# Sums of squares along rows of x on ScalarE for token groups two to eight, in a hybrid attention and retention layer

## The chip, the cores and the metric

The kernel runs on one core of a Trainium2 chip. The core has a matrix engine (TensorE, PE in the profile), a vector engine (VectorE, DVE), an activation engine (ScalarE, ACT), a general engine (GpSimd, POOL) and a queue engine (SyncE, SP) that issues most transfers between HBM and the on-chip memory SBUF. TensorE writes its results to another on-chip memory, PSUM. PEld is TensorE's loading of weights. Each engine works through its own instructions in order and waits on semaphores for the others. The metric is the time of one execution on the device, in microseconds (us); lower is better.

## The reference, cut to what matters

One layer works on 2048 latent tokens x and 256 context tokens ctx, each of 1024 channels:

```python
mod = jax.nn.silu(c) @ w_ada[i] + b_ada[i]             # the same for c_ctx
shift, scale, gate = mod[:, None, :D], mod[:, None, D:2 * D], mod[:, None, 2 * D:]
h_lat = _rmsnorm(x, norm_g[i]) * (1.0 + scale) + shift  # x * rsqrt(mean(x*x) + EPS) * g
h_ctx = _rmsnorm(ctx, norm_g[i]) * (1.0 + scale_c) + shift_c
y_lat, y_ctx = _mixer(h_lat, h_ctx, w_in[i], ...)       # projections, attention, retention
x = x + gate * y_lat
return _rmsnorm(x, final_norm_g)
```

What matters here is the first normalisation: for each token the sum of the squares of its 1024 channels, from it a reciprocal root, and then h = x * root * A + B with A and B per channel, from `mod`. h goes into all the input projections.

## The kernel before, in words

**Tokens and tiles.** The tokens are cut into nine groups of 256: groups 0 to 7 are x, group 8 is ctx. The host hands x over in two layouts. In `xT` (and `ctxT`) channels are on the 128 partitions and tokens along the row, eight channel slices k 0 to 7; h is made from this one, because TensorE needs the channels on the partitions. In `x` (and `ctx`) tokens are on the partitions and channels along the row; before the change only the end of the kernel reads that one. Two groups make a block of 512 tokens, `blk[b]`: a high part (`hhi`) and a low part (`hlo`, what the rounding of the high part leaves out). Each projection is three matmuls per slice k: high by high weight, low by high weight, high by low weight (`tform`, L363).

**The windows.** `window(b)` makes four projection units of block b, step by step: 32 steps per window, three matmuls in each. In window 0 `STEPS` interleaves the four units; later windows take one unit after the other. Each finished unit is copied from PSUM by ScalarE and DVE (L383, L384) and stored to `kS` by SP. Windows 0 to 3 are x, window 4 is ctx. Window 0 has the adaLN matmuls (`ada_mm`, L311) between its steps: four column quarters u, each of four parts j.

**The plan.** `PLAN` is a list written out by hand: (step, action, arguments). After the matmuls of step n (32 per window, counted through) `run_acts(n)` issues the actions whose step is n, in the order of the list. So PLAN sets the order on every engine. Actions with step -1 come before window 0. They are:

- `x` i: request xT of group i (two transfers of 512 KB); `sq` i: squares of group i and their sums over the slices (`squares`, L198 to L203); `cs`: TensorE sums over the partitions, one column per 128 tokens, by matmuls with a vector of ones (`colsum`, L209);
- `rs` i: mean and EPS on DVE (L214), power -0.5 on POOL (L215), and a copy along the row on DVE (L220); `sp`: TensorE turns it so that each token's root lies in its column on all partitions (`spread`, L227); `mu` i, u: DVE multiplies x by it, half u of the slices (L241);
- `ab` i, u: times A plus B per slice, some on DVE (L272) and some on ScalarE (L274), by `TSQ`; `blk` b: take the tiles of block b; `hl` i, u: ScalarE casts the high half (L279), DVE or POOL subtracts for the low one (L283), by `LOV`;
- `p` k: slice k of h for groups 0 and 1 at once (`prep_first`, L262 to L265);
- `s`, `m`, `ar`, `af`: split a part of the adaLN weights (L298, L300), its matmuls (L311), the copy of a finished row of quarter u (L319: ScalarE for even u, DVE for odd u), and its transposes and A and B (L324 to L332);
- `ws`, `w`, `w2`: split or request weights of the projections.

**Buffers and queues.** The pool `st` has four tiles of 512 KB. They hold raw weights, the squares of groups 2 to 8 (two each), and ctx. A tile is handed on in list order as it becomes free; the next writer waits until its last reader is done. Before window 0 the list `LOADS` fills SP's queue: x of groups 0 to 3, the adaLN weights and two sets of projection weights. Each x that has been turned into h is stored to `hS` (`spill_step`, L253), from eight steps after its `hl`, one store at an odd step; the tiles of x of groups 0 and 1 become block 2's high part, those of groups 2 and 3 its low part, so `hl` of groups 4 and 5 waits for these stores. All of these are on SP's queue, and it issues in order: a transfer that waits for its tile holds up those after it.

## Time and profile before

| | |
|---|---|
| median of three runs | 1360.33 us (1356.68 to 1361.18) |
| the profiled execution, its time | 1357.68 us |
| the profiled execution, its span | 1355.7 us |
| TensorE busy | 1310.1 us, 97% |
| DVE, ScalarE, POOL busy | 61%, 45%, 43% |
| mean granted clock of TensorE | 0.996 |
| DMA | 287.25 MB, 212 GB/s |

A row of the timeline gives the start, the length, the engine, the line of the kernel, the operation with its tiles, and in brackets how long the engine stood idle before it and what ended that. A row of the groups gives the same operation summed: the count, the busy time in us, the mean length in ns, and the idle time before. A row of the stages gives, for a stretch of time, the busy us of PE, PEld, DVE, ACT and POOL, the granted clock of TensorE (1.00 is full speed), the DMA share and GB/s. Matmuls are pipelined and their ends are modelled, so the start of the next one says more than the length of one.

### The profile page before, as it was taken

How to read it: one execution, taken by the hardware profiler on the slowest of the kernel's cores; microseconds unless marked ns; L12 is line 12 of the kernel's file. 1: busy time of each engine (PE TensorE's matmuls, PEld its weight loads, DVE VectorE, ACT ScalarE, POOL GpSimd, SP SyncE). 2: the span in 40 equal slices, each digit the busy share in tenths (PEclk: the TensorE clock that was granted, in tenths of full speed). 3: DMA queues.
4: the chain of work that ended last, by engine and by line, in shares of the span. 5: the costliest groups of instructions: out<-in, count | busy, mean ns of one | idle time of the engine just before them, and what ended most of it. 6: DMA issues, size and time to landing. Idle time of an engine off the chain costs nothing.

```text
span 1355.7 us, 23094 instructions
## 1 busy us (share of the span) xinstructions
PE 1310.1 (97%) x8236; PEld 1146.9 (85%) x8236; DVE 828.3 (61%) x1444; ACT 606.5 (45%) x1259; POOL 579.9 (43%) x569
## 2 busy tenths in 40 slices
PE   6999999999999999999999999999999899999997
PEld 2477899887897788998999889889999789888886
DVE  5687366676766755377767777776654633445345
ACT  4454343343533344455555465556643244333432
POOL 4443101554034664445535474655523154544442
PEclk9999999999999999999999999999999999999999
DMA  9386788464867656978587886666528888555433
GB/s 363 135 279 231 259 313 215 164 210 147 326 182 230 216 203 213 265 210 211 148 225 207 226 224 206 195 181 193 163 90 291 278 290 279 159 163 171 163 121 129
DMA packets 172085, 287.25 MB, mean 212 GB/s; under 512 B 17345, under 2 KB 92225, under 8 KB 170690
## 3 DMA queue, kind: packets, MB, share of 16 engines
q1 hardware_dynamic: 139554, 228.35, 55.8%
q10 hardware_dynamic: 32416, 57.42, 11.8%
q8 instruction: 66, 1.08, 0.3%
q14 instruction: 49, 0.40, 0.1%
HBM read 194.48 MB, written 91.23 MB: 211 GB/s over the span
## 4 chain that ended last, share of the span: by engine, by line
PE 70%; DVE 9%; DMA 8%; POOL 4%; issue 4%; ACT 3%; SPq 1%; ACTq 0%; DVEq 0%; POOLq 0%
PE mm L374 17%; PE mm L671 12%; PE mm L1463 11%; PE mm L363 7%; PE sS L1025 4%; PE tr L1052 3%; PE po L1073 3%; PE mm L1187 2%; PE mm L311 2%; PE tr L1054 2%; PE po L1075 2%; DMA v<-rvS 1%; PE mm L1375 1%; POOL hlo L531 1%; PE mm L1374 1%
## 5 line engine op out<-in xcount | busy, mean ns | idle before, releaser
L374 PE MATMUL mm<-whi,hlo 128*128 128x256 f32 x832 | 228.6, 282 | 1.0 <-DMA hlo<-cS 1.0
L374 PE MATMUL mm<-whi,hhi 128*128 128x256 f32 x768 | 224.3, 292 | 0.0
L374 PE MATMUL mm<-wlo,hhi 128*128 128x256 f32 x768 | 216.8, 282 | 0.0
L1056 ACT CAST pt<-tr 128x640 fp32r<-128x640 f32 (+1 forms) x128 | 95.6, 747 | 160.4 <-PE tr L1054 157.8
L1062 DVE TENSOR_TENSOR pt<-tr,pt 128x640 fp32r<-128x640 f32 (+1 forms) x128 | 114.0, 890 | 78.4 <-ACT pt L1056 77.2
L374 PEld LDWEIGHTS mm<-whi,hlo 128*128 128x128 f32 x832 | 156.6, 191 | 1.4 <-DMA hlo<-cS 1.3
L1045 POOL TENSOR_SCALAR sp<-sp,stt 128x640 f32<-128x640 f32 (+2 forms) x128 | 103.1, 808 | 106.3 <-DVE stt L1044 75.7
L374 PEld LDWEIGHTS mm<-whi,hhi 128*128 128x128 f32 x768 | 146.3, 191 | 0.0
L374 PEld LDWEIGHTS mm<-wlo,hhi 128*128 128x128 f32 x768 | 146.1, 190 | 0.0
L1034 DVE CUSTOM_DVE_ANT_0 sp<-sS,nb 128x640 f32<-128x640 f32 (+2 forms) x128 | 105.6, 825 | 33.4 <-DMA nb<-in_rpb_t_dram 20.7
L1039 ACT ACTIVATE sp<-sp,stt 128x640 f32<-128x640 f32 (+2 forms) x128 | 107.4, 839 | 20.3 <-DVE stt L1034 19.1
L625 POOL TENSOR_TENSOR whi<-st,whi 128x512 fp32r<-128x512 f32 x48 | 62.8, 1330 | 107.7 <-ACT whi L624 107.7
L363 PE MATMUL mm<-hhi,whi 128*128 128x512 f32 x256 | 108.2, 423 | 0.0
L363 PE MATMUL mm<-hlo,whi 128*128 128x512 f32 x256 | 102.0, 399 | 6.0 <-DVE hlo L265 2.1
L1025 PE MATMUL sS<-k,q 128*128 128x256 f32 (+3 forms) x512 | 99.1, 315 | 5.1 <-DVE stt L1034 4.7
L363 PE MATMUL mm<-hhi,wlo 128*128 128x512 f32 x256 | 102.0, 398 | 0.3 <-DVE wlo L347 0.3
L671 PE MATMUL mm<-hhi,whi 128*128 128x512 f32 x336 | 98.1, 395 | 1.6 <-POOL whi L625 1.6
L1463 PE MATMUL mm<-wor,y 128*128 128x512 f32 x384 | 95.7, 398 | 1.1 <-DVE xt L1472 1.1
L1472 DVE TENSOR_TENSOR xt<-mm,xt 128x512 f32<-128x512 f32 x64 | 43.9, 687 | 82.6 <-PE mm L1463 82.5
L1025 PEld LDWEIGHTS sS<-k,q 128*128 128x128 f32 x512 | 82.8, 188 | 12.0 <-DVE stt L1034 8.2
L1463 PE MATMUL mm<-won,y 128*128 128x512 f32 x336 | 89.9, 406 | 0.0
L625 POOL TENSOR_TENSOR wlo<-st,wlo 128x512 fp32r<-128x512 f32 x36 | 53.1, 1476 | 75.8 <-ACT wlo L624 73.7
(258 smaller groups left out, 3051.5 us busy)
## 6 DMA issues: line engine op xcount, KB each, us to landing
st<-in_w_in_dram SPq DMA_DIRECT2D x64, 512.0 KB
q<-qS SPq DMA_DIRECT2D x64, 256.0 KB
hlo<-hS SPq DMA_DIRECT2D x20, 512.0 KB
k<-kS SPq DMA_DIRECT2D x16, 576.0 KB
kS<-o SPq DMA_DIRECT2D x16, 512.0 KB
vB<-o SPq DMA_DIRECT2D x64, 128.0 KB
qS<-o ACTq DMA_DIRECT2D x16, 512.0 KB
woS<-g ACTq DMA_DIRECT2D x32, 256.0 KB
```

What stands on the lines that cost most here:

```text
L363: nc.tensor.matmul(pm[:, :n], ww[:, k, cs], h[:, k, :], start=(k == 0 and i == 0), stop=(k == KC - 1 and i == 2))
L374: nc.tensor.matmul(pm[:, t * WG:(t + 1) * WG], h[:, k, o:o + P], ww[:, k, :], start=(k == 0 and i == 0), stop=(k == KC - 1 and i == 2))
L625: nc.gpsimd.tensor_tensor(t[:, 1], r, f(t)[:, 0], ALU.subtract)
L671: nc.tensor.matmul(pm, ww[:, k, :], hh[:, k, :], start=(k == 0 and i == 0), stop=(k == KH - 1 and i == 2))
L1025: nc.tensor.matmul(o, hd["q"][i][:, hl, j * P:(j + 1) * P], k, start=(hl == 0), stop=(hl == 1))
L1034: nc.vector.tensor_tensor_reduce(T["sp"][:, :n], T["s"], nbz[big][:, o:o + n], -1.0, 3e38, ALU.add, ALU.min, T["st"][:, 0:1])
L1039: nc.scalar.activation(sp[:, :n], sp[:, :n], AF.Exp, bias=st[:, 0:1], scale=-1.0, accum_out=st[:, 1:2])
L1045: nc.gpsimd.tensor_scalar(sp[:, :n], sp[:, :n], st[:, 2:3], 0.0, ALU.mult, ALU.add)
L1056: nc.scalar.copy(pt[:, :ng_ + 2, 0, :], tr[:, :ng_ + 2, :])
L1062: nc.vector.tensor_tensor(pt[:, :n, 1, :], tr[:, :n, :], f(pt)[:, :n, 0, :], ALU.subtract)
L1463: nc.tensor.matmul(pm, yy[:, k, :], ww[:, k, sl], start=(k == 0 and i == 0), stop=(k == 3 and i == 2))
L1472: nc.vector.tensor_tensor(xts[t][:, sl], pm, xts[t][:, sl], ALU.add)
```

## The change

Groups 2 to 8 get their sums of squares in another way. A new action `xt` i requests the group's rows from `x` (or `ctx`), token on the partition, in two transfers of 512 KB into two `st` tiles. `sq` i for these groups is now two ScalarE instructions, Square with an accumulated sum along the row, which leave the sums of 128 tokens each in a column of a small SBUF tile `rs`. The adds on DVE and POOL (L200 to L203) and the column sums on TensorE (L209) stay for groups 0 and 1 alone. `rs` works on that tile in place.

```diff
+    def load_xt_(i):
+        sqs[i] = []
+        src = a["ctx"] if i == 8 else a["x"][i * 256:(i + 1) * 256, :]
+        for t in range(2):
+            xt = env["st"].tile([P, KH, 256], F32, name="st").rearrange("p k t -> p (k t)")
+            nc.sync.dma_start(xt, src[t * P:(t + 1) * P, :])
+            sqs[i].append(xt)
+
     def squares(i):
+        if i >= 2:
+            rms[i] = env["st"].tile([P, 2], F32, name="rs", bufs=4)
+            for t, xt in enumerate(sqs[i]):
+                nc.scalar.activation(xt, xt, AF.Square, accum_out=rms[i][:, t:t + 1])
+            return
         sqs[i] = []
         for u in range(2):
-            sq = xsq[i][u] if i < 2 else env["st"].tile([P, KH, 256], F32, name="st")
+            sq = xsq[i][u]
...
     def rstd(i):
-        r = env["st"].tile([P, 2], F32, name="rs", bufs=4)
+        r = rms[i] if i >= 2 else env["st"].tile([P, 2], F32, name="rs", bufs=4)
```

The plan changes with it, from step 4 on. The rows of groups 2 and 3 are requested right behind `LOADS`, ahead of x of groups 4 and 5; the other rows follow as tiles become free. The `sq` of groups 2 and 3 stand at step 9, ahead of the row copy `ar` 2; before, group 2 stood at step 5 (ahead of `p` 3) and group 3 at step 12. The `rs` and `sp` of groups 2 and 3 come at steps 12 and 13 (before: 15 and 16), and all of block 1's `mu`, `ab` and `hl` at steps 13 to 22, ahead of `p` 7 and `p` 6 in part (before: 17 to 29). ctx is requested at step 32 (before: 79), its rows at step 46. From step 53 on, the actions other than squares, column sums and requests keep their steps.

```diff
-    (-1, 'p', 0), (-1, 'p', 1), (-1, 'm', 1, 3), (-1, 'ws', 1), (0, 'ar', 1), (3, 'af', 1), (4, 'mu', 1, 1),
-    (4, 's', 2, 0), (4, 'x', 4), (4, 'p', 2), (5, 'sq', 2), (7, 'm', 2, 0), (8, 'm', 2, 1), (9, 'p', 3),
-    (9, 'm', 2, 2), (9, 'm', 2, 3), (9, 'ar', 2), (12, 'mu', 0, 1), (12, 'af', 2), (12, 'm', 3, 0), (12, 'sq', 3),
-    (12, 'p', 5), (12, 'm', 3, 1), (12, 'p', 4), (13, 'sq', 4), (13, 'cs', 2, 3), (13, 'm', 3, 2), (14, 'm', 3, 3),
-    (15, 'rs', 2), (15, 'ar', 3), (16, 'rs', 3), (16, 'af', 3), (16, 'sp', 2, 3), (17, 'mu', 3, 0), (18, 'p', 7),
-    (19, 'mu', 2, 0), (20, 'x', 5), (20, 'p', 6), (22, 'mu', 2, 1), (23, 'mu', 3, 1), (23, 'cs', 4), (24, 'ab', 2, 0),
...
-    (31, 'sq', 5), (34, 'mu', 4, 1), (39, 'ab', 4, 0), (42, 'cs', 5), (42, 'rs', 5), (48, 'ab', 4, 1), (50, 'sp', 5),
+    (-1, 'p', 0), (-1, 'p', 1), (-1, 'm', 1, 3), (-1, 'ws', 1), (0, 'ar', 1), (3, 'af', 1), (4, 'xt', 2),
+    (4, 'xt', 3), (4, 'mu', 1, 1), (4, 's', 2, 0), (4, 'x', 4), (4, 'p', 2), (7, 'm', 2, 0), (8, 'm', 2, 1),
+    (9, 'p', 3), (9, 'sq', 2), (9, 'sq', 3), (9, 'm', 2, 2), (9, 'm', 2, 3), (9, 'ar', 2), (10, 'xt', 4),
+    (10, 'x', 5), (11, 'xt', 5), (12, 'mu', 0, 1), (12, 'af', 2), (12, 'm', 3, 0), (12, 'p', 5), (12, 'm', 3, 1),
+    (12, 'p', 4), (12, 'rs', 2), (12, 'rs', 3), (13, 'sp', 2, 3), (13, 'm', 3, 2), (13, 'mu', 2, 0), (13, 'mu', 3, 0),
+    (14, 'm', 3, 3), (14, 'sq', 4), (14, 'ab', 2, 0), (14, 'blk', 1), (14, 'ab', 3, 0), (14, 'hl', 2, 0),
+    (15, 'ar', 3), (15, 'mu', 2, 1), (15, 'xt', 6), (16, 'af', 3), (16, 'hl', 3, 0), (16, 'mu', 3, 1), (17, 'p', 7),
+    (18, 'p', 6), (19, 'ab', 2, 1), (19, 'rs', 4), (20, 'ab', 3, 1), (20, 'sq', 5), (21, 'hl', 2, 1), (21, 'xt', 7),
+    (22, 'hl', 3, 1), (26, 'sp', 4), (26, 'x', 6), (28, 'mu', 4, 0), (30, 'mu', 4, 1), (31, 'sq', 6), (32, 'x', 8),
+    (36, 'ab', 4, 0), (40, 'rs', 5), (42, 'ab', 4, 1), (45, 'sq', 7), (46, 'xt', 8), (48, 'sp', 5), (50, 'mu', 5, 0),
...
+    (55, 'hl', 4, 0), (55, 'hl', 5, 0), (55, 'ab', 5, 1), (60, 'sq', 8), (61, 'hl', 5, 1), (62, 'rs', 6),
+    (68, 'sp', 6), (70, 'rs', 7), (73, 'mu', 6, 1), (73, 'ab', 6, 1), (73, 'hl', 6, 1), (75, 'sp', 7),
```

## The prediction

> **What bounds the kernel now.** I read the busy shares first, then the stages of the first 165 us, then TensorE's idle times there, and last the groups of instructions that the change takes out.

> ```profile
> span 1355.7 us, 23094 instructions
> PE 1310.1 (97%) x8236; PEld 1146.9 (85%) x8236; DVE 828.3 (61%) x1444; ACT 606.5 (45%) x1259; POOL 579.9 (43%) x569
> ```

> TensorE sets the end: 97% busy. The change touches the first five windows alone (0 to about 160 us), so it is worth what it takes from TensorE's idle time, slow clock and extra matmuls there; all later work follows TensorE. By the matmul rows, window 0 runs from 28 to 74 us, window 1 from 74.2, window 2 from 101.2. The idle times (in brackets) that matter:

> ```profile
> 38.46 0.50 PE L363 MATMUL mm<-hlo,whi 128*128 128x512 f32 x1 [1.73 <-DVE hlo L265]
> 49.24 0.41 PE L324 MATMUL mm<-ident,o 4*128 4x4 f32 x4
> 53.92 0.95 PE L209 MATMUL mm<-one,st 128*128 128x1 f32 x8
> 54.79 1.88 PE L311 MATMUL mm<-clo,silc 128*2 128x512 f32 x4
> 61.24 1.33 PE L227 MATMUL mm<-ident,t 128*128 128x128 f32 x8
> 67.27 0.47 PE L363 MATMUL mm<-hlo,whi 128*128 128x512 f32 x1 [0.37 <-DVE hlo L265]
> 76.55 0.47 PE L363 MATMUL mm<-hlo,whi 128*128 128x512 f32 x1 [1.96 <-DVE hlo L283]
> 103.04 0.50 PE L363 MATMUL mm<-hlo,whi 128*128 128x512 f32 x1 [1.45 <-POOL hlo L283]
> 108.47 0.71 PE L227 MATMUL mm<-ident,t 128*128 128x128 f32 x4 [1.51 <-DVE t L220]
> 110.75 0.58 PE L209 MATMUL mm<-one,st 128*128 128x1 f32 x4 [0.17 <-DVE st L203]
> 126.07 0.58 PE L209 MATMUL mm<-one,st 128*128 128x1 f32 x4 [0.15 <-DVE st L203]
> ```

> The stages (busy time of PE, PEld, DVE, ACT, POOL; then TensorE's granted clock, DMA share, GB/s):

> ```profile
> 30.00:40.00 10.00, 7.96 (x33) 4.45 (x32) 8.73 (x13) 4.98 (x8) 8.05 (x5) 0.99 1.03 410
> 40.00:50.00 10.00, 10.00 (x28) 3.58 (x27) 2.87 (x6) 2.48 (x3) 2.09 (x2) 0.84 0.52 206
> 50.00:60.00 10.00, 10.00 (x33) 3.65 (x32) 8.40 (x17) 3.97 (x6) 5.18 (x7) 1.00 0.00 1
> 60.00:70.00 10.00, 9.63 (x50) 7.59 (x49) 8.58 (x18) 5.01 (x10) 3.09 (x4) 1.00 0.00 0
> 70.00:80.00 10.00, 8.04 (x33) 6.28 (x32) 9.19 (x14) 8.45 (x12) 7.28 (x4) 0.86 0.61 183
> 80.00:90.00 10.00, 10.00 (x46) 8.29 (x45) 6.62 (x12) 2.58 (x5) 2.34 (x3) 0.96 1.05 383
> 90.00:100.00 10.00, 10.00 (x48) 8.36 (x47) 9.13 (x12) 6.94 (x10) 5.11 (x4) 1.00 1.03 336
> ```

> The reader is to see three things. The clock falls just after the two longest idle times: 0.84 over 40 to 50 us is a loss of about 1.6 us, and 0.86 with 0.96 after 76.5 us is 1.4 + 0.4 = 1.8 us; after 1.45 and 1.51 us of idle it did not fall. DMA is idle from 45 to 72 us, and full from 74 to 100 us. And DVE is the busy helper (8 to 9 of 10 us) wherever TensorE waits.

> **What is removed.** Seven groups lose their sums of squares on DVE and POOL and their column sums on TensorE:

> ```profile
> L200 POOL TENSOR_TENSOR st<-st 128x512 f32<-128x512 f32 x7 | 10.4, 1484 | 12.9 <-ACT st L198 12.9
> L201 POOL TENSOR_TENSOR st<-st 128x256 f32<-128x256 f32 x7 | 5.8, 832 | 0.5
> L200 DVE TENSOR_TENSOR st<-st 128x512 f32<-128x512 f32 x7 | 5.8, 833 | 0.8 <-ACT st L198 0.8
> L201 DVE TENSOR_TENSOR st<-st 128x256 f32<-128x256 f32 x7 | 3.8, 545 | 0.2
> L203 DVE TENSOR_TENSOR st<-st 128x256 f32<-128x256 f32 x7 | 3.0, 425 | 1.1 <-DVE st L201 0.5
> L209 PE MATMUL mm<-one,st 128*128 128x1 f32 x28 | 3.6, 237 | 0.3 <-DVE st L203 0.3
> ```

> Per group that is 1.80 us of DVE (0.83 + 0.55 + 0.43) and 2.32 us of POOL. On TensorE the eight column sums at 53.92 hold up the next matmul until 54.79, 0.87 us, so a group's four cost about 0.44. All seven: 7 x 0.4 = 2.8 us, straight on the path.

> **What is added.** ScalarE squares as much as before (two 128x1024 per group, 1.05 us each) and also reads an accumulator: 14 x 0.187 us = 2.6 us, hidden, since ScalarE is 45% busy.

> ```profile
> L198 ACT ACTIVATE st<-hlo 128x1024 f32<-128x1024 f32 x4 | 4.0, 1045 | 0.0
> L1419 ACT ACTIVATION_READ_ACCUMULATOR ot<-xt x32: 185/187/224, 1160.8 to 1349.9; 128x1 f32 x32
> ```

> The rows of x are 14 more transfers of 512 KB (7 MB) on SP's queue. At 410 GB/s one takes 1.28 us. Four MB of them fall into the idle 45 to 72 us. What they cost is order, on three queues, in the terms below.

> **Window 0, term by term.** (a) Squares of group two were at step 5, between two steps that feed TensorE; their adds ran on POOL and DVE while DVE made the low half that TensorE awaits at 38.46.

> ```profile
> 34.35 0.40 DVE L263 TENSOR_SCALAR hhi<-hhi,mods 128x256 f32<-128x256 f32 x1
> 36.11 1.37 DVE L263 TENSOR_SCALAR hhi<-hhi,mods 128x256 f32<-128x256 f32 x1
> 37.52 0.90 DVE L265 TENSOR_TENSOR hlo<-hhi 128x256 fp32r<-128x256 f32 x1
> ```

> Without them it is ready near 37.0: the 1.37 us falls to the 0.40 of the same operation before, and the 0.90 to the 0.43 that L203 takes for this size. Gain 1.73 - 0.3 = 1.4, and the slow clock after it, 1.6: together 3.0.

> (b) ScalarE now squares groups two and three *ahead of* the copy of the third modulation row, and waits there for rows that are requested only after all the first loads.

> ```profile
> 31.89 4.11 SPq L190 DMA_DIRECT2D hhi<-in_xT_dram x4
> ```

> The loads before end near 45.1 us (206 GB/s over 40 to 50 is five full us), with x of groups four and five last, these 2 MB; so the old list without these ends at 40.0, and the four transfers of rows two and three at 45.1. With 0.8 us until ScalarE sees it (chosen between 0 and 2), the last square with its read ends at 47.1 and the row copy at 47.7.

> ```profile
> 47.12 0.57 ACT L319 COPY o<-mm 4x512 f32<-4x512 f32 x1 [9.82 <-PE mm L311]
> ```

> So the copy is where it was, but TensorE, 3.0 us earlier by (a), reaches its transposes at 49.24 - 3.0 = 46.2 and waits 1.4. Behind the waiting ScalarE stands nothing but this copy.

> (c) The spread matmuls of groups two and three (61.24 in the old order) come forward to step 13, in place of the column sums at 53.92. Their scales stand on DVE behind the preparation of k 5 and 4 of block 0: the transposes end at 48.0, the modulation rows take DVE 0.7 us, two casts of ScalarE 0.6 each, then DVE four TENSOR_SCALARs (0.4 to 0.6, behind the casts) and two subtractions (0.4 to 0.9), to about 52.4; then per group DVE, POOL, DVE:

> ```profile
> L262 ACT ACTIVATE hhi<-hhi,mods 128x256 fp32r<-128x256 f32 x16 | 8.4, 590 | 12.4 <-DVE mods L332 8.5 <-DVE hhi L241 3.8
> L215 POOL TENSOR_TENSOR rs<-rs,mhalf 128x2 f32<-128x2 f32 x9 | 6.4, 707 | 25.8 <-DVE rs L214 25.8
> L220 DVE COPY t<-rs 128x256 f32<-128x256 f32 x9 | 3.7, 412 | 7.4 <-POOL rs L215 7.4
> L241 DVE TENSOR_TENSOR hhi<-hhi,mm 128x1024 f32<-128x1024 f32 x8 | 9.6, 1210 | 0.5 <-PE mm L227 0.5
> ```

> 1.25 us each, ready at 53.7 and 54.9. TensorE is there at 52.3: it waits 1.4 + 0.7 = 2.1.

> (d) Block 1 is made at once: between the spread and k 6 of block 0 DVE now has four multiplications by the spread (1.21), four pairs of TENSOR_SCALAR (0.4 each), a row copy, a subtraction (1.2) and k 7 and 6 (2.4), about 11.5 us from 55.5, plus 0.5 us of waits: k 6 is ready near 67.5. TensorE is there near 66 and waits 1.5 where it waited 0.37: a loss of 1.1. POOL's low halves of group two run under it.

> Window 0: +3.0 (a) + 0.87 + 0.4 (column sums of groups two, three, four) - 1.4 - 2.1 - 1.1 = -0.3. It ends as late as before; what was won early is waited away.

> **Window 1.** Block 1 is ready by about 72.5, so the 1.96 at 76.55 and the 1.8 of slow clock go: +3.8. The column sums of groups five and six go: +0.8. TensorE reaches window 2 4.2 us earlier, near 97.0.

> **Window 2.** Here the queues decide. SP is in order, and the rows of group seven wait for group five's squares, near 69 us; eight stores of x to hS, five kS stores, x of group six, ctx, then the rows of ctx stand behind: 10.5 MB, of which 9.0 until the last store that frees block 2's low half.

> ```profile
> 72.48 0.63 SPq L151 DMA_DIRECT2D kS<-o  x1
> L283 POOL TENSOR_TENSOR hlo<-hhi 128x1024 fp32r<-128x1024 f32 x2 | 5.7, 2862 | 2.6 <-ACT hhi L279 2.6
> ```

> (Before, that train began at 72.48.) At 410 GB/s the slot is free at 93 us, at the 360 of the rows for 80 to 100 us at 96; two POOL subtractions (2.4 to 2.9 each) follow: 97.8 to 101.0. I take 99.4, a wait of 2.3. ScalarE's squares of ctx wait for rows landing at 97 to 100.6, and the high half of group five's second part is queued behind them: low half 101.4 to 105.1, taken 103.2, a wait of 1.1; then the scales of group six, 1.25 us, a wait of 0.6. Sum 4.0 against 1.45 + 1.51 = 3.0 before: -1.0. DVE and POOL, relieved by 1.8 and 2.3 us per group, would alone have removed both. The last two column sums and their waits give 0.9 + 0.3 = +1.2.

> **Sum.** -0.3 + 3.8 + 0.8 - 1.0 + 1.2 = 4.5 us earlier at window 4, where TensorE has no wait but 1.0 us until 240 us, so it passes to the end. The profiled execution took 1357.68 us; this gives 1353.2. The median shown, 1360.33, lies 2.65 above that execution, and less 4.5 gives 1355.8. The four executions shown spread over 4.5 us, so I take a value between: 1355.0. About 0.3% (4.1 us) is what a measurement of this kernel can tell from no change.

> **Rivals.** (1) *The waits are exchanged, and the clock falls again* (23%): 2.1 us of idle within 3.2 us at (c), and 2.3 at window 2, are as long as those that cost 1.6 to 1.8 before. At (c) part hides in (d), so 1.3 + 1.7 = 3.0 is lost again; gain 1.5, 1358.8 by the median, within 0.3%. For it: the clock fell after 1.73. Against it: not after 1.51, and (c) is in two pieces.

> (2) *The helpers' relief wins* (22%): rows land when needed, block 2 waits for nothing. Without (b), (c)'s first wait and window 2's 4.0 the gain is 4.5 + 1.4 + 1.4 + 4.0 = 11.3; half of it, 8 to 9, is likelier: 1351.5. For it: DMA is empty for 27 us. Against it: ScalarE takes (b)'s rows in order.

> (3) *Slower: the DMA train of window 1* (11%). At the mixed rate of one early microsecond of that train,

> ```profile
> 77.00:78.00 1.00, 1.00 (x5) 0.81 (x4) 1.00 (x2) 1.00 (x2) 1.00 (x1) 0.65 0.91 263
> ```

> 10.5 MB from 69 us land at 111; squares 2.3, cast 1.05, subtraction 1.2, scales 1.25 later the spread of group six starts at 117.7 instead of 108.47: 9.2 later, less the 1.2 of window 3: 8.0 slower, 1368.3. It decides once those rows land after 104 us (break-even) and shows beyond 108.

> (4) *The slow clock does not hang on the two waits* (6%): it falls at 40 us among thin adaLN matmuls and at 77 wherever the first dense window begins, and falls in the new order too. Then the 1.6 and 1.8 stay lost: gain 4.5 - 3.4 = 1.1, 1359.2. For it: two cases are few. Against it: both follow the longest waits within 1 us, and elsewhere neither thin nor dense matmuls are slow. [...]

> (5) That rows summed on ScalarE are not what runs has no support: the same form is in the trace at L1419.

> **Numbers.** Forecast 38% (own range 1352 to 1357.5), rivals (1) to (4) 23, 22, 11 and 6%. Faster by over 0.3%: rival 2 and some 60% of the forecast, 0.45. Within: rivals 1 and 4 and the rest, 0.44. Slower: 0.11. Range 1349.5 to 1361: the unknown rows (DMA 360 or 410 GB/s, +-1.6; the clock, 3.0; (b) to (d), +-2) and most of rivals 1 and 2.

> **What would show it.** Right: no L209 beyond eight instructions; no idle before the low-half matmul that opens window 1, and a clock of 1.00 there; a wait of TensorE on ScalarE's row copy before 48 us; waits on the scale copies near 53 us; window 2 opening on POOL's low half near 99 us. Wrong: ScalarE squaring group two before 43 us, no wait at step 13, k 6 in time, or squares of ctx that wait beyond 104 us.

## The result, and the profile after

The changed kernel took 1365.21 us (median of five runs, 1364.89 to 1368.2) against 1358.52 us for the kernel before (five runs): a ratio of 1.0052, 95% interval 1.0034 to 1.0071. It is about 7 us slower where 4.5 us faster was forecast. The profiled execution took 1365.21 us. In the changed kernel the line numbers have moved: `tform` is L377, the copies of a finished unit L397 and L398, the stores of k L152 and of x to `hS` L267, `hl` L293 and L297, `ab` L286 and L288, `rs` L228 to L234, `spread` L241, the weight splits L359 and L361.

The page's first lines, then TensorE's idle times of the changed kernel:

```profile
span 1363.4 us, 23026 instructions
PE 1308.8 (96%) x8208; PEld 1146.7 (84%) x8208; DVE 814.1 (60%) x1423; ACT 607.8 (45%) x1273; POOL 563.1 (41%) x555
```

```profile
37.30 0.50 PE L377 MATMUL mm<-hlo,whi 128*128 128x512 f32 x1 [0.31 <-DVE hlo L279]
48.15 0.41 PE L338 MATMUL mm<-ident,o 4*128 4x4 f32 x4 [1.62 <-ACT o L333]
54.41 0.71 PE L241 MATMUL mm<-ident,t 128*128 128x128 f32 x4 [1.43 <-DVE t L234]
55.60 0.71 PE L241 MATMUL mm<-ident,t 128*128 128x128 f32 x4 [0.48 <-DVE t L234]
68.69 0.47 PE L377 MATMUL mm<-hlo,whi 128*128 128x512 f32 x1 [1.38 <-DVE hlo L279]
94.31 1.19 PE L241 MATMUL mm<-ident,t 128*128 128x128 f32 x4 [7.43 <-DVE t L234]
107.38 0.50 PE L377 MATMUL mm<-hlo,whi 128*128 128x512 f32 x1
111.50 0.71 PE L241 MATMUL mm<-ident,t 128*128 128x128 f32 x4 [0.51 <-DVE t L234]
...
172.80 0.38 PE L388 MATMUL mm<-whi,chi 128*128 128x256 f32 x1 [1.09 <-ACT whi L359]
174.06 0.39 PE L388 MATMUL mm<-wlo,chi 128*128 128x256 f32 x1 [0.76 <-DVE wlo L361]
```

Stages of the changed kernel (columns as in the prediction):

```profile
40.00:50.00 10.00, 8.38 (x28) 3.13 (x28) 0.67 (x4) 5.87 (x11) 0.00 (x0) 1.00 1.03 410
70.00:80.00 10.00, 10.00 (x48) 8.33 (x47) 7.70 (x8) 2.39 (x4) 2.66 (x2) 1.00 0.68 224
80.00:90.00 10.00, 6.88 (x31) 5.37 (x29) 0.98 (x2) 3.58 (x7) 0.00 (x0) 1.00 1.00 316
90.00:100.00 10.00, 5.68 (x19) 4.73 (x20) 6.75 (x14) 5.38 (x11) 0.70 (x1) 0.66 1.02 325
```

TensorE did less work, as it was to do (28 matmuls fewer). The opening of window 1 is free of waits and the clock there is 1.00. Then comes one wait of 7.43 us, for the scales of group five, and a clock of 0.66 over 90 to 100 us. The trace's clock records have TensorE at half clock from 91.47 to 98.30 us, that is 3.4 us of clock. But 2.84 us of it lie inside the wait, so the matmuls behind the wait lose only about 2.0. Together that is about 9.4 us in the middle of window 1, where the prediction had nothing. Window 1 took 31.8 us here (75.16 to 106.95); in e12 below, which has neither wait nor slow clock in it, it took 22.2.

The chain behind it is read on three engines. SyncE's issues:

```profile
69.88 0.39 SPq L267 DMA_DIRECT2D hS<-hlo  x1
76.18 0.63 SPq L152 DMA_DIRECT2D kS<-o  x1
76.86 1.86 SPq L267 DMA_DIRECT2D hS<-hlo  x1
78.81 1.44 SPq L191 DMA_DIRECT2D chi<-in_xT_dram  x2
80.86 0.60 SPq L152 DMA_DIRECT2D kS<-o  x1
...
93.03 1.99 SPq L267 DMA_DIRECT2D hS<-hlo  x2
```

ScalarE, over the same stretch:

```profile
73.25 1.05 ACT L293 CAST hhi<-hlo 128x1024 fp32r<-128x1024 f32 x1 [2.87 <-DVE hlo L286]
74.20 1.07 ACT L397 CAST o<-mm 128x512 fp32r<-128x512 f32 x2
80.37 0.58 ACT L397 CAST o<-mm 128x512 fp32r<-128x512 f32 x1 [5.10 <-DMA kS<-o]
...
89.09 0.58 ACT L397 CAST o<-mm 128x512 fp32r<-128x512 f32 x1 [6.06 <-DMA kS<-o]
...
100.35 2.95 ACT L293 CAST hhi<-hhi 128x1024 fp32r<-128x1024 f32 x3 [2.13 <-DMA hS<-hhi]
```

Before the change, the first of these copies (L383 there) waited for TensorE alone, and ran five microseconds earlier (DVE's half of it at 71.77, against 75.47 after):

```profile
69.15 0.59 ACT L383 CAST o<-mm 128x512 fp32r<-128x512 f32 x1 [1.44 <-PE mm L363]
```

And DVE in the changed kernel:

```profile
70.35 2.80 DVE L286 TENSOR_SCALAR hlo<-hlo,mods 128x256 f32<-128x256 f32 x2
...
89.71 0.69 DVE L398 TENSOR_TENSOR o<-mm,o 128x512 fp32r<-128x512 f32 x1 [8.04 <-ACT o L397]
...
92.84 0.16 DVE L228 TENSOR_SCALAR rs<-rs 128x2 f32<-128x2 f32 x1
93.87 0.29 DVE L234 COPY t<-rs 128x256 f32<-128x256 f32 x1 [0.88 <-POOL rs L229]
```

Read from the top. With all of block 1 made at once, the cast of group three's second half (73.25) stands on ScalarE ahead of the copy of the first finished unit (74.20). So the first store of k leaves at 76.18 instead of 72.48, and SyncE, which issues in order, stands still from 70.3 until then. The stores of x and the 1 MB of x 6 then go out ahead of the second store of k. The copies go into the pool `op`, which has two tiles, so the fourth copy waits until the second store has landed: 80.86 to about 89. DVE does its half of that copy right behind ScalarE and stands 8.04 us. Behind it in DVE's order are the scales of group five (92.84, 93.87), and TensorE's spread at step 48 needs them.

The second half of the same delay is paid later in SyncE's queue: the last stores of x that free block 2 go out from 92.53 to 95.0. Block 2's casts wait for the one of 92.53, from the tile `hhi`, and begin at 100.35. This is hidden in the changed kernel only because TensorE is itself late.

Three landmarks split the 7.7 us between the two profiled executions (1355.7 and 1363.4). Window 4 (ctx) begins at 153.0 before and 154.4 after: 1.4 us. The first matmul of the later stage with summed weights (called the tail below) begins at 234.3 and 238.9: 3.2 us more, lost inside the stage over ctx, where the two waits for `whi` and `wlo` above and two of 0.36 and 0.76 at 191.7 and 193.0 stand (before, only 0.51 there). From there to the end it is 1121.4 and 1124.5: 3.1 us more, in instructions that did not change.

### The profile page after: what moved, and what is told of

Read it like the earlier page. It is cut to its first block, busy times and chain, and to the rows that moved or that the text cites. A ratio compares the mean times of both kernels' runs of the same rounds, so it can differ in the third digit from the quotient of the medians.

```text
span 1363.4 us, 23026 instructions
## 1 busy us (share of the span) xinstructions
PE 1308.8 (96%) x8208; PEld 1146.7 (84%) x8208; DVE 814.1 (60%) x1423; ACT 607.8 (45%) x1273; POOL 563.1 (41%) x555
## 3 DMA queue, kind: packets, MB, share of 16 engines
q8 instruction: 65, 1.06, 0.3%
## 4 chain that ended last, share of the span: by engine, by line
PE 44%; DMA 6%; POOL 6%; DVE 5%; issue 4%; ACT 3%; ACTq 0%; SPq 0%; POOLq 0%; DVEq 0%
PE mm L1477 11%; PE mm L388 10%; PE sS L1039 4%; PE tr L1066 3%; PE mm L377 3%; PE po L1087 3%; PE mm L1201 2%; PE tr L1068 2%; PE po L1089 2%; DMA woS<-g 1%; DMA v<-rvS 1%; PE mm L1389 1%; PE mm L1388 1%; PE mm L1387 1%; POOL g L773 1%
## 5 line engine op out<-in xcount | busy, mean ns | idle before, releaser
L377 PE MATMUL mm<-hhi,whi 128*128 128x512 f32 x256 | 108.2, 423 | 0.0
L377 PE MATMUL mm<-hlo,whi 128*128 128x512 f32 x256 | 102.0, 398 | 2.1 <-DVE hlo L279 1.7
L377 PE MATMUL mm<-hhi,wlo 128*128 128x512 f32 x256 | 102.0, 399 | 0.3 <-DVE wlo L361 0.3
L1477 PEld LDWEIGHTS mm<-wor,y 128*128 128x128 f32 x384 | 69.9, 188 | 18.4 <-issue 3.5
```

Source lines behind the costliest of these rows:

```text
L377: nc.tensor.matmul(pm[:, :n], ww[:, k, cs], h[:, k, :], start=(k == 0 and i == 0), stop=(k == KC - 1 and i == 2))
L1477: nc.tensor.matmul(pm, yy[:, k, :], ww[:, k, sl], start=(k == 0 and i == 0), stop=(k == 3 and i == 2))
```

## The experiments

All ratios are to the kernel before, with 95% intervals; it had a median of 1358.52 us beside the changed kernel, and of 1359.4 to 1359.8 us beside the experiments. The last columns are the start of window 4, of the tail, and the distance between, each from the profiled execution. No kernel leaves out any of the computation.

| kernel | ratio | window 4 | tail | between |
|---|---|---|---|---|
| before | 1 | 153.0 | 234.3 | 81.3 |
| changed | 1.0052 [1.0034, 1.0071] | 154.4 | 238.9 | 84.5 |
| e1 | 1.0066 [1.0042, 1.0090] | 157.4 | 242.6 | 85.2 |
| e2 | 1.0106 [1.0077, 1.0135] | 161.0 | 247.7 | 86.7 |
| e3 | 1.0027 [1.0011, 1.0043] | 155.2 | 237.2 | 82.0 |
| e4 | 1.0071 [1.0043, 1.0099] | 160.6 | 243.5 | 82.9 |
| e5 | 1.0038 [1.0022, 1.0055] | 154.9 | 240.9 | 86.0 |
| e6 | 1.0015 [0.9999, 1.0030] | 150.8 | 238.0 | 87.2 |
| e7 | 1.0067 [1.0043, 1.0091] | 156.2 | 243.3 | 87.1 |
| e8 | 1.0019 [0.9999, 1.0039] | 153.2 | 236.1 | 82.9 |
| e9 | 1.0001 [0.9984, 1.0019] | 153.3 | 234.3 | 81.0 |
| e10 | 0.9986 [0.9966, 1.0005] | 150.4 | 231.9 | 81.5 |
| e11 | 1.0058 [1.0035, 1.0080] | 155.1 | 242.1 | 87.0 |
| e12 | 1.0034 [1.0018, 1.0051] | 155.5 | 235.9 | 80.4 |
| e13 | 0.9998 [0.9983, 1.0013] | 151.9 | 233.7 | 81.8 |
| e14 | 1.0020 [1.0008, 1.0032] | 154.4 | 235.5 | 81.1 |
| e15 | 1.0015 [1.0000, 1.0031] | 154.8 | 235.6 | 80.8 |
| e16 | 1.0043 [1.0028, 1.0057] | 156.7 | 238.3 | 81.6 |
| e17 | 0.9988 [0.9973, 1.0003] | 150.8 | 232.1 | 81.3 |
| e18 | 0.9978 [0.9963, 0.9992] | 149.1 | 230.4 | 81.3 |

### e1: the scales of group five out of the wait

```diff
-    (40, 'rs', 5)
+    (22, 'rs', 5)
```

> The changed kernel with the scales of group five (rs 5) at step 22 in place of 40, so that DVE does them before it waits for any copy of a finished unit. Theory A (SP's one queue: stores of x to hS stand behind kS stores, so block 2's tiles come free late, at 100.4 us): the 7.4 us wait before the spread of group five goes, but TensorE then waits at the opening of window 2 for the low half that POOL ends near 107 us; time within 2 us of the changed kernel's 1365. Rival B (only the place of rs 5 in DVE's order): 7.4 us of idle and 3.4 us at half clock go, 1355.

Measured: 1367.43 us, 0.4 us above what theory A allowed. The wait of 7.43 is gone, and TensorE's idle times in the timeline of e1 now are:

```profile
105.97 0.80 PE L377 MATMUL mm<-hhi,whi 128*128 128x512 f32 x1 [7.61 <-ACT hhi L293]
109.90 0.80 PE L377 MATMUL mm<-hlo,whi 128*128 128x512 f32 x1 [3.13 <-POOL hlo L297]
```

The scales were late only because DVE stood in the copy. Taking them out does not help, because block 2 is late from the same cause: its casts wait for a store of x (ScalarE, 2.80 us at 102.98).

### e2: the stores of k on ScalarE's own queue

```diff
-            if b == 4 and n == 0:
+            if b == 0 and n == 0:
                 env["queue"] = nc.scalar
```

> The changed kernel with the kS stores of windows 0 to 3 issued by ScalarE's queue in place of SP's. Theory A: SP no longer stands behind copies that are not done, the hS stores go out at their steps (before 80 us, in place of up to 95), block 2's tiles are free before 93 us, no wait over 2 us in windows 1 and 2; 1353 to 1356. Rival C (7 MB more for the DMA engines, whatever the order): the waits stay, 1363 to 1366.

Measured: 1373.86 us, the slowest of all and outside both ranges; the expected gain did not come. ScalarE's timeline in e2:

```profile
84.68 0.59 ACT L397 CAST o<-mm 128x512 fp32r<-128x512 f32 x1 [6.46 <-DMA kS<-o]
```

SyncE no longer stands still: it issues stores of x from 70.64 to 78.88. But the first store of k is issued at 76.96 (76.18 in the changed kernel), among them, and the third copy waits for its landing until 84.68. ScalarE now also waits for DVE's half of a copy before it can issue the store, up to 5.27 us at a time. So the place in SyncE's queue is only a part of the cause, and e2 brought a cost of its own; it does not tell the two apart.

### e3 and e4: rows without the new order, the new order without rows

e3 keeps rows and sums on ScalarE, but puts the scales and all of h of groups two to four back at the old steps. e4 keeps the sums of the kernel before (groups three and five are squared earlier) and makes the block at once. Of each edit some entries are shown.

```diff
e3:
-    (13, 'mu', 2, 0), (14, 'ab', 2, 0), (14, 'hl', 2, 0), (22, 'hl', 3, 1)
+    (19, 'mu', 2, 0), (24, 'ab', 2, 0), (28, 'hl', 2, 0), (29, 'hl', 3, 1)
...
e4, against the kernel before:
-    (16, 'sp', 2, 3), (19, 'mu', 2, 0), (24, 'ab', 2, 0), (29, 'hl', 3, 1)
+    (13, 'sp', 2, 3), (13, 'mu', 2, 0), (14, 'ab', 2, 0), (22, 'hl', 3, 1)
```

> Rows and ScalarE sums as in the changed kernel, but scales, multiplications and h of groups two to four at the steps they had before (15 to 48), so h of block 1 is not made at once. If the rows are the cause (rival C): a wait of 5 us or more in window 1 or 2 stays, 1362 or more. If making h at once is the cause (it puts block 1's last casts ahead of the first copy of a unit, so the first kS store and all behind it go out 3.7 us later): no such wait, the 2 us at the opening of window 1 come back, 1356 to 1360.

> The kernel before with its sums on DVE, POOL and TensorE, but the steps of the changed kernel for groups two to five: h of block 1 at once, squares of group three at step 9, of five at 20. No rows are loaded. If making h at once delays the first kS store and the train behind it (theory A): a wait of over 4 us for group five's scales or at the opening of window 2, 1361 or more. If the rows are the cause (rival C): neither wait, 1354 to 1358.

Measured: e3 1363.64 us, e4 1367.34 us. TensorE's timeline in e4:

```profile
97.27 1.20 PE L227 MATMUL mm<-ident,t 128*128 128x128 f32 x4 [8.11 <-DVE t L220]
```

e4 has the wait, without one row loaded. So the order of h makes it, and the 7 MB of rows are not needed for it. e3 has no such wait, but it does not come back to the kernel before either: 1356 to 1360 was expected, and its ratio is 1.0027 [1.0011, 1.0043]. Its window 1 opens with waits of 1.07 and 1.48 us and a clock of 0.81 and then 0.85, much as in the kernel before, and at 104.20 and 108.71 us it waits 2.02 and 1.68 us for block 2. The second of these is the one that the prediction's account of window 2 had: ScalarE stood 3.47 us for the rows of ctx, and a cast of block 2 stood behind. So the rows have a cost of their own, smaller than that of the order.

### e5 and e8: copies that need not wait for a store

Window 0's four copies get four tiles that lie idle by then, instead of the two of `op`; e8 does the same in the kernel before.

```diff
-        o = op.tile([P, 2, 512], F32R, name="o")
+        o = wad[8 + own.pop(0)].bitcast(F32R) if b == 0 else op.tile([P, 2, 512], F32R, name="o")
```

> The changed kernel, where the four copies of window 0's finished units go to four tiles that are free then (those of the adaLN weights of quarter 2), not to the two that each kS store must leave first. Theory D (the fourth copy waits for the landing of the second kS store, DVE waits in order for that copy, and group five's scales and SP's stores behind the fourth kS store wait with it): the 8.0 us idle of DVE and the 7.4 us of TensorE go, the last stores that free block 2 go out before 90 us in place of 95; 1352 to 1358. Rival E (the DMA engines are full from 78 us, the landing only shows it): a wait of over 5 us moves to the opening of window 2, 1362 or more.

> The kernel before with the four copies of window 0's units in tiles of their own as in e5. There ScalarE waits 4.0 us for a landing before the fourth copy (83.09), but TensorE waits for nothing behind it; theory D: within 2 us of the kernel before, as what bounds it is DVE between 92 and 107 us.

Measured: e5 1364.45 us (rival E's time), e8 1361.18 us. In e5 DVE's 8 us at the fourth copy are gone, and ScalarE and TensorE read:

```profile
99.08 2.94 ACT L293 CAST hhi<-hhi 128x1024 fp32r<-128x1024 f32 x3 [9.77 <-DMA hS<-hhi]
```

```profile
102.07 0.79 PE L377 MATMUL mm<-hhi,whi 128*128 128x512 f32 x1 [4.53 <-ACT hhi L293]
106.00 0.80 PE L377 MATMUL mm<-hlo,whi 128*128 128x512 f32 x1 [3.14 <-POOL hlo L297]
```

The shared tiles make the first wait, and the late train of stores makes the second; removing one shows the other. In the kernel before, neither bites: its waits stayed as they were (1.97 and 1.45).

### e6: the first copy ahead of the second halves

```diff
-    (19, 'ab', 2, 1), (20, 'ab', 3, 1), (21, 'hl', 2, 1), (22, 'hl', 3, 1)
+    (25, 'ab', 2, 1), (25, 'ab', 3, 1), (25, 'hl', 2, 1), (25, 'hl', 3, 1)
```

> The changed kernel with the second halves of block 1 (ab and hl, half 1, of groups two and three) at step 25, behind the copy of the first finished unit (step 24), in place of steps 19 to 22. Theory D with its start in the crowding: the first copy runs near 72 us in place of 74.2 and the first kS store near 73 in place of 76.2, so the fourth copy waits about 3 us less; TensorE's wait falls from 7.4 to 3 to 5 us, a wait of up to 2 us for block 1's second half comes at step 36; 1359 to 1364. If the crowding is not the start: as the changed kernel, 1365.

Measured: 1360.76 us. The first store of k goes out at 72.71, and window 4 begins at 150.8, 2.2 us ahead of the kernel before. TensorE's idle times in e6:

```profile
91.07 0.68 PE L241 MATMUL mm<-ident,t 128*128 128x128 f32 x4 [2.96 <-DVE t L234]
...
171.15 0.58 PE L388 MATMUL mm<-whi,chi 128*128 128x256 f32 x1 [3.06 <-ACT whi L359]
172.41 0.58 PE L388 MATMUL mm<-wlo,chi 128*128 128x256 f32 x1 [0.46 <-DVE wlo L361]
```

So what stands ahead of the first copy starts the chain. And what was won there was lost again in the stage over ctx, with a clock of 0.66 over 170 to 180 us: the second loss, larger here than in the changed kernel.

### e7: x of group six later

```diff
-    (26, 'x', 6)
+    (44, 'x', 6)
```

> The changed kernel with x of group six (1 MB) requested at step 44 in place of 26, so it does not stand between the first and the second kS store on SP. Theory D: the second kS store goes out some 1.5 us earlier and lands some 3 us earlier, the fourth copy and TensorE's wait shrink by 3 us; 1360 to 1363. If the landing does not decide: 1365.

Measured: 1367.69 us (theory D: 1360 to 1363). TensorE's wait at the scales of group five falls to 3.18 us, but 2.28 and 0.76 us and smaller ones come up after 104 us, and 3.1 in the stage over ctx. ScalarE stands 4.08 us for the rows of ctx at 106.33 there. That the moved request is what delays them was not tested by itself.

### e9, e10, e14: the second loss

In the stage over ctx the copies of window 4 again wait for stores of k. Behind them on ScalarE is the split of the next weights. ScalarE in the changed kernel:

```profile
168.10 0.37 ACT L397 CAST o<-mm 128x256 fp32r<-128x256 f32 x1 [4.26 <-DMA kS<-o]
...
170.28 0.37 ACT L397 CAST o<-mm 128x256 fp32r<-128x256 f32 x1 [1.80 <-DMA kS<-o]
...
171.70 1.99 ACT L359 CAST whi<-st 128x1024 fp32r<-128x1024 f32 x2 [1.05 <-DVE o L398]
```

The kernel before has one such wait there, a shorter one:

```profile
165.83 0.37 ACT L383 CAST o<-mm 128x256 fp32r<-128x256 f32 x1 [3.27 <-DMA kS<-o]
```

At that time SyncE reads 2 MB of h back (`hhi` from `hS`, issued at 156.55 in the changed kernel). The edit puts these four requests behind the next request for weights, which waits for its tiles, so they go out at 165.57 in e14; e9 has it on the kernel before, e14 on the changed one, e10 on e6.

```diff
-            if b == 4 and n % 8 == 0:
-                raw_piece(0, n // 8)
...
     load_w()
+    for n in range(4):
+        raw_piece(0, n)
     w0 = wr[3]
```

> The kernel before, with one edit: the four requests that read 2 MB of stored h back (hhi from hS, issued by SyncE at 155.2 to 157.6 in the kernel before, while the stores of k of the window over ctx go out) stand behind the request for weights that SyncE holds until 172.5. Theory A (the read-back slows the stores of k, whose landing holds ScalarE's copies, and these hold the split of the next weights): ScalarE's waits for kS landings in that window fall from 3.27 us to under 1.5, the wait of 0.51 for whi at 171.1 goes, and the time falls by 0.5 to 1.5 us, unless the read-back is now late for its first use at 188.3. Rival C (stores and weights are late for another reason): those waits stay within 0.5 us and the time is the same.

> The changed kernel with the second halves of groups two and three behind the first copy (as in e6) and the read-back of h behind the held request for weights (as in e9). Window 4 should begin at 150.8 as in e6, 2.2 us before the kernel before. Theory A: TensorE's waits of 3.06 and 0.46 for whi, and the slow clock over 170 to 180, go; the tail begins 3 to 4 us earlier than in e6 (234 instead of 238) and the time falls from 1360.8 to 1356 to 1358, under the kernel before. Rival C (what is won ahead of window 4 is lost there in any case, because the weights come when they come): a wait of 2 us or more for whi stays, and the time stays within 1 us of 1360.8.

> The changed kernel with the read-back of h behind the held request for weights (as in e9) and nothing else. It sizes the second loss by itself: window 4 should begin at 154.4 as in the changed kernel. If what was lost behind window 4 (84.5 us from its start to the tail, against 81.3 before) comes from the read-back, the waits of 1.09, 0.76, 0.36 and 0.76 for whi go, the distance to the tail falls to 81 to 82 and the time by 2.5 to 3.5 us, to 1361.5 to 1363; what stays over the kernel before is then window 1's share. If it does not come from there: the distance stays at 84 or more and the time is 1365.

Measured: e9 1359.18 us, e10 1357.09 us (not to be told from the kernel before), e14 1362.72 us. TensorE in e10:

```profile
90.72 1.19 PE L241 MATMUL mm<-ident,t 128*128 128x128 f32 x4 [3.03 <-DVE t L234]
...
174.32 0.38 PE L388 MATMUL mm<-wlo,chi 128*128 128x256 f32 x1 [0.67 <-DVE wlo L361]
```

The distance from window 4 to the tail falls from 87.2 to 81.5 (e6 to e10) and from 84.5 to 81.1 (changed to e14). In all nine kernels that have the edit it lies between 80.4 and 81.8; without it, between 81.3 and 87.2. In e14 the same copy of ScalarE, at 166.11, waits 2.16 us for TensorE and no longer for a store. So the read-back is what takes the 3.2 us, and theory A holds where there was something to lose. In e9 the wait for the store goes too, but the kernel before lost only 0.51 us there and the time stays (0.5 to 1.5 us less was expected). Why its weights are in time behind a wait of 3.27 us, and those of the changed kernel late, was not tested.

### e11 and e12: with ctx moved back as well

Both have e5's and e6's edits and ctx at the old steps; e12 has the later read-back too.

```diff
-    (32, 'x', 8), (46, 'xt', 8), (60, 'sq', 8)
+    (79, 'x', 8), (80, 'xt', 8), (86, 'sq', 8)
```

> The changed kernel with three edits: second halves of groups two and three behind the first copy (e6), window 0's copies into tiles of their own (e5), and the requests and sums for ctx (x 8, xt 8, sq 8) back at the steps of the kernel before (79, 80, 86). Theory A (the chain of late stores and the two shared copy tiles cause the first loss, whole): no wait over 1 us on TensorE between 75 and 120, and window 4 begins at 149 to 150.5. The time then depends on what the stage over ctx gives back: with waits for whi of 3 to 5 us as in e6, 1358 to 1361. Rival: a wait of over 2 us stays somewhere between 75 and 120, because the order of h itself leaves too much work ahead of each unit; time 1360 to 1364.

> e11 with the read-back of h behind the held request for weights as in e9 and e10. Theory A in both places: no wait over 1 us between 75 and 120, none for whi over 0.5 us after 160, and the forecast's gain arrives: 1353 to 1356, against about 1359.5 for the kernel before. Rival C: the wait for whi stays and the time is that of e11 within 1 us.

Measured: 1366.59 and 1363.7 us, both outside every range. Half of theory A's expectation came: no wait over 0.9 us from 75 to 120 us, and window 1 at its shortest, 22.2 us. The other half did not, because of this edit itself. TensorE and ScalarE in e12:

```profile
128.81 0.80 PE L377 MATMUL mm<-hhi,whi 128*128 128x512 f32 x1 [6.13 <-ACT hhi L293]
```

```profile
123.65 1.06 ACT L207 ACTIVATE st<-st 128x1024 f32<-128x1024 f32 x1 [6.75 <-DMA st<-in_ctx_dram]
```

Rows that are requested six steps ahead hold ScalarE for 6.75 us, and the casts of block 3 stand behind. Sums on ScalarE from their own copy of the rows need the early request. The sums of the kernel before, from the tiles that x is in anyway, don't.

### e13, e15, e16: both causes removed, and ctx between the trains

e13 is e10 with e5's tiles. e15 is e13, and e16 is e10, with ctx at other steps:

```diff
-    (32, 'x', 8), (46, 'xt', 8), (60, 'sq', 8)
+    (64, 'x', 8), (64, 'xt', 8), (80, 'sq', 8)
```

> The changed kernel with three edits: second halves of groups two and three behind the first copy (e6), window 0's copies into tiles of their own (e5), the read-back of h behind the held request for weights (e9); the rows of ctx stay at the changed kernel's steps (32, 46, 60). Theory A: the wait of 3.03 us for group five's scales and the 1.7 us of half clock behind it, which e10 keeps, go too; no wait over 1.5 us between 75 and 240; window 4 begins at 146 to 149 and the tail at 227 to 231; time 1351 to 1355, faster than the kernel before. Rival D (with own tiles the stores of the second block of h become the next limit, as in e5): a wait of 2 to 5 us at the opening of window 2 takes the place of the one removed, window 4 begins at 150 to 152, time 1356 to 1359.

> e13 with the four requests for ctx (2 MB) at step 64 instead of 32 and 46, and the sums over its rows at step 80 instead of 60: SyncE then sends them at about 108, behind the stores of the second block of h, and ten steps ahead of their use. Theory A (in e13 the train of requests on SyncE between 72 and 98 is the limit, and ctx's 2 MB stand in it): the stores of h end by 93 instead of 96, the waits of 1.07 and 3.44 us at the opening of window 2 fall under 1 us together and the half clock behind them goes; ScalarE's wait for ctx rows stays under 1 us (6.75 in e12, which asked for them at step 80); window 4 begins at 147 to 149.5 and the time falls by 2.5 to 4.5 us from e13's 1358.15 to 1353.5 to 1355.5. Rival: the same wait comes back at the sums over ctx, or the place of the requests does not matter: time 1357 to 1361.

> The same move of ctx on e10, which has no tiles of its own for window 0's copies. Theory A: the wait of 3.03 us for group five's scales stays within 1 us, since the copies that hold it wait for the stores of k ahead of ctx in the train; the time is that of e10 (1357.1) within 1.5 us. Rival: if ctx's place alone carried the loss, that wait goes as well and the time falls to 1354 or less.

Measured: e13 1358.15 us, e15 1360.96 us, e16 1364.65 us. Rival D was right for e13, whose window 2 opens with waits again and half clock behind them. TensorE and the stage in e13:

```profile
99.20 0.50 PE L377 MATMUL mm<-hhi,whi 128*128 128x512 f32 x1 [1.07 <-ACT hhi L293]
103.14 0.80 PE L377 MATMUL mm<-hlo,whi 128*128 128x512 f32 x1 [3.44 <-POOL hlo L297]
```

```profile
100.00:110.00 10.00, 6.86 (x20) 5.57 (x21) 6.73 (x10) 4.35 (x7) 4.48 (x4) 0.66 0.84 316
```

In e15 these go, as expected, but ctx now delays the stores for block 3. ScalarE and TensorE in e15:

```profile
118.68 1.05 ACT L293 CAST hhi<-chi 128x1024 fp32r<-128x1024 f32 x1 [8.88 <-DMA hS<-hhi]
```

```profile
127.80 0.66 PE L377 MATMUL mm<-hhi,whi 128*128 128x512 f32 x1 [4.30 <-ACT hhi L293]
```

e16 keeps its wait for group five's scales (3.15 us; expected within 1 us of 3.03) and has the new one (3.85 us) as well; its time is outside what theory A gave. At both places that were tried, stores that somebody waited for stood behind the 2 MB and were late.

### e17 and e18: 2 MB out of the trains

x of groups six and seven are requested right behind the last use of the tiles that they fill, where the transfers were nearly idle (58 GB/s over 60 to 70 us in e13). e17 is e13 with this, e18 is e10 with it.

```diff
-    (26, 'x', 6), (53, 'x', 7)
+    (14, 'x', 6), (14, 'x', 7)
```

> e13 with the requests for x 6 and x 7 (2 MB) at step 14, behind the last use of the tiles they fill: SyncE then sends them at about 61.5, where e13 moves only 58 GB/s (60 to 70), instead of at 73.4 and 95.8 inside the train of stores of k and h. ctx stays at 32 and 46. Theory A (every megabyte in the train before 98 delays the stores behind it by about 2.7 us at 376 GB/s): the last store of h's second block goes out about 2 us earlier than at 91.1, the waits of 1.07 and 3.44 us at the opening of window 2 fall under 2 us together and the half clock behind them goes; window 4 begins at 148 to 150 and the time falls from 1358.15 to 1354 to 1356. Rival: the stores are held by their copies and not by the bytes ahead of them; the waits stay within 0.7 us and the time within 1.5 us of e13, or the time is above it because the sums over rows, asked for behind x 7, come late.

> The same move on e10. Theory A: the copies of window 0 wait for stores of k that have 1 MB less ahead of them; ScalarE's wait of 6.81 us at 85.40 falls to 4 to 5, TensorE's wait of 3.03 us for group five's scales to under 1 us, without the half clock; time 1353 to 1355.5, faster than the kernel before. Rival: that wait stays within 0.7 us and the time within 1.5 us of 1357.1.

Measured: e17 1358.65 us (ratio 0.9988), e18 1357.88 us (0.9978 [0.9963, 0.9992]). TensorE in e18:

```profile
88.41 0.68 PE L241 MATMUL mm<-ident,t 128*128 128x128 f32 x4 [1.44 <-DVE t L234]
...
102.11 0.50 PE L377 MATMUL mm<-hlo,whi 128*128 128x512 f32 x1 [2.54 <-POOL hlo L297]
```

The wait for the scales falls from 3.03 to 1.44 (under 1 was expected) with no half clock behind it (1.00 over 90 to 100, against 0.83), ScalarE's wait for the landing from 6.81 to 3.76 us (4 to 5 was expected). The bytes ahead of the stores thus set a good part of that wait. The time did not follow: 1353 to 1355.5 was expected, and it is within 1 us of e10's, as the rival had it. e18's window 4 begins 3.9 us and its tail 3.9 us ahead of the kernel before, but its median is only 2.0 us lower. It is the one kernel here whose interval lies below the kernel before. As the best of eighteen, and at 0.2% where the prediction takes 0.3% for the least that can be told, it is not a gain that is shown. Against the changed kernel it is clear: 0.9978 and 1.0052 of the kernel before, about 10 us. In e17 one wait of 3.45 us stays at the opening of window 2, with the half clock (0.66 over 100 to 110): without the wait for tiles TensorE arrives earlier (98.28, against 99.17 in e18) and waits for the same low halves in one piece, so there theory A missed and the rival's time came.

## Why the prediction was wrong

**Window 0 came out step by step.** (a) The wait for the low half is 0.31 (0.3 was forecast), and the clock over 40 to 50 us is 1.00. (b) The transposes wait 1.62 (1.4). (c) The spread waits 1.43 and 0.48 (1.4 and 0.7). (d) k 6 is late by 1.38 (1.5), at 68.69. Window 0 took 46.9 us instead of 46.2, 0.7 more where 0.3 was forecast. Window 1 opens without a wait and at full clock, as forecast, and rival (4), by which the clock falls at 40 and 77 us in any case, is out.

That (a) and (b) came out so well was luck. The half clock of rival (1) did not come in this execution. Sixteen profiled kernels have window 0 in this form up to (b). In eleven of them the half clock came behind it: the eight matmuls that follow (`mm<-chi,silc`) take 5.26 to 6.47 us there, against 3.59 or 3.60 in the changed kernel, e2, e5 and e12; of e6 only the wait was read. TensorE and a stage of e13:

```profile
48.25 0.58 PE L338 MATMUL mm<-ident,o 4*128 4x4 f32 x4 [3.01 <-ACT o L333]
```

```profile
50.00:60.00 10.00, 10.00 (x27) 3.02 (x26) 6.97 (x15) 5.37 (x12) 2.95 (x4) 0.78 0.81 323
```

In the sixteen the wait at (b) runs from 1.59 us (e5) to 3.67 (e6), half of them above 2.6, so the forecast's 1.4 was too short in all. Both sides scatter: window 0 opens between 27.00 and 28.37 us, and ScalarE's first square begins between 42.53 and 43.72. The changed kernel's profile has a late opening and early rows. So the 1.6 us of clock that (a) won here was lost again in most of the others.

**The step that failed is "Window 1 ... TensorE reaches window 2 4.2 us earlier".** It counted what goes there, and nothing that comes. It reached window 2 at 107 instead of 101.2, 5.8 us later: 10 us from the forecast. The prediction followed ScalarE, DVE and POOL up to the low halves of block 1, but not the copies of window 0's units, which stand behind them on ScalarE, the two tiles that these copies share, and the scales of group five behind them on DVE. It priced the order of block 1 at step (d), by k 6, and asked there only what TensorE awaits in window 0. e4 shows that this order makes the wait without the rows, e6 that the place of the copy sets it off, e5 that the shared tiles carry it to DVE, and e18 that the bytes ahead of the stores set part of its length. The rows of the change are a second, smaller cost (e3).

**Window 2's account failed with it.** The prediction let the train start at 69 us and saw in the row of 72.48 only a start that comes sooner; but that row is the store that SyncE stands still for, and it came at 76.18. Its waits of 2.3, 1.1 and 0.6 were 0, 0 and 0.51 in the changed kernel, because TensorE was late itself. From window 2 to window 4 the changed kernel gained 4.4 us (5.8 late to 1.4 late) where 0.2 was forecast. The column sums and the waits of 1.45 and 1.51 that go there make 4.2 together, when nothing is paid for them. e1 and e5 show that price: 4.5 to 7.6 and 3.1 us at the opening.

**"So it passes to the end" failed too.** The stage over ctx had only 1.0 us of idle, but its ScalarE waits 3.27 us for a store there, and the split of weights is just in time. The changed kernel lost 3.2 us in it and e6 5.9. e10 and e14 take these away by moving 2 MB of read-back. A stage with no idle time is not one with slack: the row of the copy's wait would have said so.

**Rival (3)** had the right thing, a train of transfers in window 1 that starts late or runs slow, but put it on the rows of ctx and at the spread of group six, with 8.0 us. There the wait was 0.51. It was given 11%. In e3 and e7 the rows of ctx do hold ScalarE, for 3.47 and 4.08 us, but at the casts of block 2.

**What stays open.** The last 3.1 us of the profiled difference lie behind the tail's start, in unchanged instructions. In the profiled executions of the twenty kernels this distance runs from 1120.5 (e10) to 1126.1 us (e14), without a relation to the edits that I could find. The changed kernel shows a clock of 0.98 over 400 to 500 and over 1000 to 1100 us where the kernel before shows 1.00: two stretches of half clock of 3.41 us, 1.7 us lost in each. They would be enough for the 3.1 us, but not for the whole scatter: e18 shows 0.98 over the same twice 100 us and has 1126.0, e10 shows 1.00 all through from 200 to 1300 us and has 1120.5, 5.5 us apart where the clock makes 3.4. What makes the rest was not tested. The scatter is also why the ratio of a kernel follows its tail start only to within 3 us.

## What to carry to other kernels

When work is moved forward on an engine that runs in order, follow everything that it is moved past until that result is used: here a copy, whose store, whose tile, whose next copy, and the small scale behind it. For an early request, look for a store behind it that somebody waits for: with ctx at step 64 a cast waited 8.88 us for such a store (e15). The one early request that shortened a wait here (3.03 to 1.44 us, e18) went into a stretch in which only 54 GB/s moved without it (60 to 70 us in e10). And before a gain is carried to the end, look in the later stages for helpers that are just in time, not for idle time of the main engine.

## What the runs showed of the hardware

So I count a wait by the part of it that lies inside one stretch, which is an estimate from these few cases. The kernel before's 1.73 and 1.96 us lie whole in one, and the clock fell. Behind (b) in the changed kernel it did not; there the 1.62 us are cut into 0.56 and 1.06. In e18 the clock of 0.99 over 40 to 50 and 0.84 over 50 to 60 us puts the start of a half-clock stretch near 49.8 us, and fifteen stretches later a border near 101.0. By this estimate the 2.54 us ahead of 102.11 are cut into about 1.4 and 1.1, and the clock there is 1.00. A stretch at half clock is 1.7 us of clock, less where TensorE waits in it: of the 6.83 us at half clock from 91.47 in the changed kernel 2.84 lie in a wait, which leaves 2.0.

**Some VectorE operations ended with GpSimd's.** Two TENSOR_SCALARs of 128x256 take 0.72 us with POOL idle (68.47 in the changed kernel) and 2.80 us while POOL subtracts (70.35, POOL from 70.45 to 73.00). One by one, the first took 0.41 us; the second began at 70.67 and ended at 73.16, just behind POOL. Of the three from 102.58, two took 2.49 us each, under two POOL operations (102.48 to 107.33), and the third 0.40 us behind them. What makes them end together is not shown. On the way to the first copy this cost 2 us that the prediction didn't have.

**Two 512 KB stores took 8.2 and 7.7 us to land.** In the changed kernel the second store of k was issued at 80.86 and its tile came free at 89.09, 8.2 us, with a DMA share of 1.00 and 316 GB/s over 80 to 90 us. In e2, where ScalarE issued, the first store of k took 7.7 us (76.96 to 84.68), at 321 GB/s over 70 to 80 and 330 over 80 to 90 us.
